# Two model blocks on one core: the weight blocks start at another byte of their 64-byte lines

## The chip, the cores and the metric

The kernel runs on one core of one Trainium2 chip. The metric is the device time in microseconds (us) of one execution. Durations of single instructions are given in nanoseconds (ns). TensorE multiplies matrices; VectorE (DVE in the profile), ScalarE (ACT) and GpSimd (POOL) work on elements; SyncE (SP) issues most DMAs.

## The reference

The reference computes two transformer-like blocks one after the other on 1024 tokens of width 1024, in 32-bit floats. Cut to what matters here:

```
u = rms_norm(x) @ w_in                   # 1024 -> 3072: RG-LRU and gated linear attention
h = x + concat(ya, yb) @ w_out
h = h + sigmoid(rms_norm(h) @ w_ple_gate + b) * (p @ w_ple_proj)
x = rms_norm(h)
z = norm(x) @ w_in_2                     # three mixers: gated attention, mLSTM, S5, and gates
y = sum of gate_b * (branch_b @ proj_b);  x = x + norm(y @ w_out_2)
x = x + norm((silu(g) * u) @ ffn_w_out), [g, u] = norm(x) @ ffn_w_in
```

Nearly all of the arithmetic is in products of the activations with large weight matrices.

## The kernel before

**Products.** Each 32-bit factor is split into a high part that TensorE's one-pass format holds (float32r) and a low part with the rest. One product of full accuracy is three matrix products, high x high, high x low and low x high (`mm3`, line 2457, all issued at line 2455). In the usual form the weight is the stationary operand, 128 x 128, loaded into the array by a LDWEIGHTS; 512 columns of the activations stream past it (the moving operand). In the profile such a product reads `mm<-rh,hi`: output, moving, stationary; `rh` and `rl` are the activations' parts, `hi` and `lo` the weight's. In a few groups (`vgroup`, line 243, and `vg` in phase B) the roles are exchanged: the activations are stationary and 256 (once 280) columns of the weight block stream.

**The ring of weight blocks.** A weight arrives as a block `raw` of 128 partitions x 1024 floats by a DMA on SP's queue; ScalarE copies it to `hi` and DVE subtracts to get `lo` (`split`, line 2466). `hi` and `lo` come from a ring of four buffers each (`ring`, line 2329), `raw` from two. The class `Stream` (line 2288) holds the list of all blocks in the order of use; when a block is used up (`done`), the next in the list is made (`more`). The ring is filled in this way in four stages that `__init__` puts into the list (line 2335): phase A (`seq_a`), phase C (`seq_c`), phase B (`seq_b`) and phase F (`seq_f`). Phase F has three kinds of keys: `"p"` (the projection), `"f"` (the first matrix of the feed-forward part, with sums and differences of blocks in a fast multiplication scheme, `variant`) and `"q"` (its second matrix, `variant2`). Within `variant` and `variant2` the ring's tiles are also filled from sums (`sl`, `sc`).

**Addresses.** In the built program each partition's row of a `hi` or `lo` buffer has 4096 bytes and begins at a multiple of 64 bytes (32192, 36288, 40384, ...), and so does every moving tile (`rh`, `rl`, `tv`, `yr`, `ah`, `al`). A product takes a slice of 128 floats (512 bytes) of the row, so its stationary block begins on a 64-byte line too. Some smaller tiles lie 32 bytes into a line: `gk` and `C` in the rows below, while `mk` and `T` of the same rows begin on one. The convolution (lines 359 to 363) reads its input rows at 0, 4, 8 and 12 bytes from their start:

```
self.act(xc, xa[:, 3 : 3 + T], AF.Identity, scale=w[3], bias=self.col("conv_b", b))
for j in (0, 1, 2):
    self.stt(xc, xa[:, j : j + T], w[j], xc, ALU.mult, ALU.add)
```

The slices that the 280-column group streams begin at 0, 1120 and 2240 bytes of a row, so one in three lies 32 bytes into a line:

```
n, per, parts = (280, 3, 3) if key == ("gv", 0) else (256, 4, 2)
c = slice((k % per) * n, (k % per) * n + n)
```

**What sets the order.** TensorE's instructions stand in the order in which the program is written (`manual_schedule`); small work of the mixers is dealt between the large products by `tick` (line 2373), one portion per 2500 ns of counted product time. The Tile layer places the waits between engines.

Of the kernel before, what the change touches and what calls it, by code (L numbers as in the profile page):

```python
# [9 lines left out]
F32R = mybir.dt.float32r  # L10
# [6 lines left out]
P = 128  # L17
# [1731 lines left out]
class PhaseF:  # L1749
# [57 lines left out]
    def variant(self, n, g, v):  # L1807

        if n == 0:
            self.fetch_raws(-1)  # L1810
        hi = self.ring.tile([P, 1024], F32R, tag="hi", name=self.name("hi"))
        lo = self.ring.tile([P, 1024], F32R, tag="lo", name=self.name("lo"))
        if v[0] == "A" and len(v) == 2:
            self.split(hi, lo, self.raws["g", 2 * g + int(v[1])])
        else:
            if v == "S1":
                self.sl[g] = self.base.tile([P, T], F32, tag="rmask", name=self.name("sl"))
            for i in range(2):
                c = slice(i * H, i * H + H)
                j = 2 * g + i  # L1820
                up, s = self.raws["u", j], self.sl[g][:, c]
                gate = self.raws.get(("g", j))
                if v == "S1":
                    self.padd(s, up[:, :H], up[:, H:])
                elif v == "S2":
                    self.psub(s, s, gate[:, :H])
                elif v == "S4":
                    self.psub(s, gate[:, H:], s)
                elif v == "S3":
                    s = self.fl.tile([P, H], F32, tag="s3", name=self.name("s3"), bufs=1)  # L1830
                    self.psub(s, gate[:, :H], up[:, :H])
                else:
                    s = up[:, H:]
                (self.psplit if g < 1 and v != "A22" else self.split)(hi[:, c], lo[:, c], s)
        self.fetch_raws(n)
        return hi, lo
# [23 lines left out]
    def variant2(self, v, e):  # L1860
        n = (2 if e < 5 else 1) * H
        if v == "S1":
            s = self.sc[e] = self.sp.tile([P, n], F32, tag=f"sc{e}", name=f"sc{e}")
            a, b = self.quad(1, 0, e), self.quad(1, 1, e, "ru")
            self.add(s, a, b)
        elif v in ("S2", "S4"):
            s, a = self.sc[e], self.quad(0, v == "S4", e)
            if v == "S2":
                self.sub(s, s, a)
            else:  # L1870
                self.sub(s, a, s)
        elif v == "S3":
            s, b = self.quad(0, 0, e), self.quad(1, 0, e, "ru")
            self.sub(s, s, b)
        else:
            s = self.quad(int(v[1]) - 1, int(v[2]) - 1, e)
        hi = self.ring.tile([P, 1024], F32R, tag="hi", name=self.name("hi"))
        lo = self.ring.tile([P, 1024], F32R, tag="lo", name=self.name("lo"))
        self.split(hi[:, :n], lo[:, :n], s)
        return hi, lo  # L1880

# [409 lines left out]
class Stream:  # L2291


    def __init__(self, k):
        self.k, self.seq, self.left = k, [], {}
        self.tiles, self.next = {}, 0

    def extend(self, seq, uses):
        self.seq += seq
        self.left.update(uses)  # L2300

    def start(self):
# [2 lines left out]

    def more(self):
        if self.next < len(self.seq):
            key, src, n = self.seq[self.next]
            self.next += 1
            self.tiles[key] = src() if callable(src) else self.k.load_split(src, n)  # L2310

# [10 lines left out]
class K(PhaseA, PhaseB, PhaseC, PhaseF):  # L2322
    depth = 4

    def __init__(self, tc, a, out):
        self.tc, self.nc, self.a, self.out = tc, tc.nc, a, out
        nc = self.nc
        self.base = tc.alloc_tile_pool(name="base", bufs=1, side="left")
        self.ring = tc.alloc_tile_pool(name="ring", bufs=self.depth, side="left")
        self.mmp = tc.alloc_tile_pool(name="mmp", bufs=4, space=PSUM)  # L2330
        self.smp = tc.alloc_tile_pool(name="smp", bufs=4, space=PSUM)
        self.ws = Stream(self)
        self.fast, self.side, self.rate, self.credit = [], [], 1.0, 0.0
        self.inside, self.ns = False, 0.0
        for s in (self.seq_a, self.seq_c, self.seq_b, self.seq_f):
            self.ws.extend(*s())

        self.edge = tc.alloc_tile_pool(name="edge", bufs=1, side="right")
        self.edge.tile([P, 8], F32, name="edge")
        self.region = tc.alloc_tile_pool(name="region", bufs=1, side="right")  # L2340
        self.uid = 0
        self.consts()
# [127 lines left out]

    def load_split(self, src, n=1024):
        raw = self.raw_tile()
        hi = self.ring.tile([P, 1024], F32R, tag="hi", name=self.name("hi"))
        lo = self.ring.tile([P, 1024], F32R, tag="lo", name=self.name("lo"))
        dst = raw[:, :n]
        if len(src.shape) == 3:
            dst = dst.rearrange("p (k c) -> p k c", k=src.shape[1])
        self.nc.sync.dma_start(dst, src)
        self.split(hi[:, :n], lo[:, :n], raw[:, :n])
        return hi, lo  # L2480

    def raw_tile(self):
        return self.ring.tile([P, 1024], F32, tag="raw", name=self.name("raw"), bufs=2)
# [94 lines left out]
```

## Time and profile before

| | |
|---|---|
| median of three runs | 2267.45 us (2266.79 to 2274.45) |
| the profiled execution | 2265.43 us, span 2263.6 us |
| TensorE busy | 2192.0 us, 10998 products |
| DVE, ScalarE, GpSimd busy | 1514.4, 903.3, 394.7 us |
| granted TensorE clock, mean | 0.986 of full |
| DMA | 297.59 MB, mean 131 GB/s |

The span runs from the first to the last instruction. Products overlap (a product's 389 ns contain the time in which its last columns run through the array), so the step from one start to the next is the measure, not the mean duration. The chain of work is followed back from the last instruction, at each step to what released it.

### The profile page before, as it was taken

Reading aid. Unit: us, or ns where it says so; the run is one execution under the profiler, and the core shown is the slowest. Engines: PE = TensorE matmul, PEld = TensorE weight load, DVE = VectorE, ACT = ScalarE, POOL = GpSimd, SP = SyncE. Lnnn points to the kernel's source line nnn. Section 1 sums busy time; section 2 is a strip of 40 time slices with the busy share of each in tenths; the row PEclk is TensorE's granted clock in tenths of the full one; section 3 lists DMA queues with packets and bytes.
Section 4 is the critical chain, followed back from the end, with each engine's and each line's share of the span. In section 5 each row is a group of like instructions: output and inputs, shape, how many; then the busy total and the mean of one; then the engine's idle time right before and its main releaser. Section 6 shows DMA issues by size and latency. Waiting matters only on the chain.

```text
span 2263.6 us, 29466 instructions
## 1 busy us (share of the span) xinstructions
PE 2192.0 (97%) x10998; PEld 1807.4 (80%) x10998; DVE 1514.4 (67%) x2160; ACT 903.3 (40%) x1522; POOL 394.7 (17%) x388
## 2 busy tenths in 40 slices
PE   8999999999999999999999999999799999999896
PEld 7888788887888988878887778887578888887676
DVE  6675686777486535558555346858977676779697
ACT  5553453344255544234253222446423232334343
POOL 1000000001112200000000000011745343425245
PEclk9999999999999999999999999999899999999998
DMA  4111116321743343255454255654233222267754
GB/s 172 34 44 40 40 51 205 103 61 29 224 144 115 98 145 136 98 170 166 152 172 143 79 183 181 202 180 153 88 123 110 84 84 84 98 228 253 246 177 160
DMA packets 149815, 297.59 MB, mean 131 GB/s; under 512 B 21520, under 2 KB 43936, under 8 KB 149416
## 3 DMA queue, kind: packets, MB, share of 16 engines
q1 hardware_dynamic: 135128, 271.33, 37.2%
q0 software_dynamic: 8128, 20.07, 2.5%
q10 hardware_dynamic: 6416, 4.31, 0.7%
q8 instruction: 87, 1.43, 0.3%
q14 instruction: 56, 0.46, 0.1%
HBM read 232.55 MB, written 61.90 MB: 130 GB/s over the span
## 4 chain that ended last, share of the span: by engine, by line
PE 76%; DVE 10%; DMA 5%; issue 5%; ACT 2%; POOL 2%; SPq 0%; POOLq 0%; ACTq 0%; DVEq 0%
PE mm L2455 56%; PE sm L2455 19%; DVE lo L2423 2%; DVE al L2423 1%; PE sm L2464 1%; DVE sc L2423 1%; DMA c<-ffa 1%; DVE res L2435 1%; DVE acc L2423 1%; POOL res L1843 1%; ACT hi L2449 0%; DVE B L2435 0%; DVE rl L2435 0%; DMA raw<-in_wfo 0%; ACT C L2449 0%
## 5 line engine op out<-in xcount | busy, mean ns | idle before, releaser
L2455 PE MATMUL mm<-rh,hi 128*128 128x512 f32 x1552 | 625.6, 403 | 1.1 <-DVE res L2423 0.7
L2455 PE MATMUL mm<-rl,hi 128*128 128x512 f32 x1552 | 606.2, 391 | 1.8 <-DVE rl L2423 1.8
L2455 PE MATMUL mm<-rh,lo 128*128 128x512 f32 x1552 | 606.7, 391 | 0.0
L2455 PEld LDWEIGHTS mm<-rh,hi 128*128 128x128 f32 x1552 | 292.5, 188 | 72.8 <-issue 9.5
L2455 PEld LDWEIGHTS mm<-rh,lo 128*128 128x128 f32 x1552 | 292.2, 188 | 62.8
L2455 PEld LDWEIGHTS mm<-rl,hi 128*128 128x128 f32 x1552 | 292.7, 189 | 61.7 <-issue 3.1
L2449 ACT ACTIVATE hi<-raw 128x1024 fp32r<-128x1024 f32 (+2 forms) x189 | 182.7, 970 | 369.3 <-PE mm L2455 265.7
L2423 DVE TENSOR_TENSOR lo<-raw,hi 128x1024 fp32r<-128x1024 f32 (+2 forms) x189 | 218.4, 1159 | 112.6 <-ACT hi L2449 110.3
L2455 PE MATMUL mm<-yr,hi 128*128 128x512 f32 x384 | 118.8, 390 | 0.2 <-DVE yr L2435 0.2
L2455 PE MATMUL mm<-tv,hi 128*128 128x512 f32 x312 | 102.5, 408 | 14.0 <-DVE tv L2423 7.1
L2455 PE MATMUL mm<-hi,rh 128*128 128x256 f32 (+1 forms) x384 | 110.7, 288 | 0.0
L2455 PE MATMUL mm<-hi,rl 128*128 128x256 f32 (+1 forms) x384 | 109.2, 284 | 0.0
L2455 PE MATMUL mm<-lo,rh 128*128 128x256 f32 (+1 forms) x384 | 109.2, 284 | 0.0
L1840 POOL TENSOR_TENSOR sl<-ru 128x512 f32<-128x512 f32 x22 | 37.1, 1689 | 315.7 <-DMA ru<-in_wfi 315.7
L2538 POOL TENSOR_TENSOR hss<-hss,mhalf 128x4 f32<-128x4 f32 x16 | 16.8, 1047 | 398.2 <-DVE hss L2441 292.1
L2455 PEld LDWEIGHTS mm<-tv,hi 128*128 128x128 f32 x312 | 61.1, 197 | 31.1 <-DVE tv L2423 9.4
L2455 PEld LDWEIGHTS mm<-yr,hi 128*128 128x128 f32 x384 | 72.1, 188 | 16.1 <-DVE yr L2435 1.1
L2449 ACT ACTIVATE hi<-sl 128x512 fp32r<-128x512 f32 x66 | 39.3, 626 | 108.9 <-PE sm L2455 66.6
L2435 DVE SCALAR_TENSOR_TENSOR adaa<-adar,cact,adaa 128x512 f32<-128x512 f32 x84 | 62.8, 747 | 29.8 <-DMA adar<-in_adaw 28.9
L2455 PEld LDWEIGHTS mm<-hi,rh 128*128 128x128 f32 x384 | 73.4, 191 | 1.7 <-issue 1.2
L2455 PE MATMUL mm<-yr,lo 128*128 128x512 f32 x192 | 74.7, 389 | 0.0
L2455 PEld LDWEIGHTS mm<-hi,rl 128*128 128x128 f32 x384 | 73.5, 191 | 0.7 <-issue 0.2
(526 smaller groups left out, 4356.7 us busy)
## 6 DMA issues: line engine op xcount, KB each, us to landing
raw<-in_w SPq DMA_DIRECT2D x60, 512.0 KB
adar<-in_adaw SPq DMA_DIRECT2D x96, 256.0 KB
c<-ffa SPq DMA_DIRECT2D x88, 256.0 KB
raw<-in_wfo SPq DMA_DIRECT2D x40, 512.0 KB
raw<-in_wfi SPq DMA_DIRECT2D x30, 512.0 KB
raw<-in_wo SPq DMA_DIRECT2D x24, 512.0 KB
ru<-in_wfi SPq DMA_DIRECT2D x22, 512.0 KB
raw<-in_wpj SPq DMA_DIRECT2D x32, 256.0 KB
```

The source lines that it names most:

```text
L1840: self.nc.gpsimd.tensor_tensor(out=out, in0=a, in1=b, op=ALU.add)
L1843: self.nc.gpsimd.tensor_tensor(out=out, in0=a, in1=b, op=ALU.subtract)
L2423: self.nc.vector.tensor_tensor(out=out, in0=a, in1=b, op=op)
L2435: self.nc.vector.scalar_tensor_tensor(out=out, in0=a, scalar=s, in1=b, op0=op0, op1=op1)
L2449: self.nc.scalar.activation(out=out, in_=a, func=f, scale=scale, **kw)
L2455: self.nc.tensor.matmul(out, lhsT=l, rhs=r, start=start, stop=stop)
L2464: self.nc.tensor.transpose(out, a, self.ident[:n, :n])
L2538: self.nc.gpsimd.tensor_tensor(out=out, in0=tmp, in1=self.mhalf[:, : out.shape[1]], op=ALU.pow)
```

## The change

The ring's tiles get 1040 floats instead of 1024, and what is used of them is a view of 1024 that begins `shift` floats in. `shift` is an entry of the stream's list. It is 4 floats (16 bytes) in phase A, 12 (48 bytes) in phase C, 2 (8 bytes) in phase B, and in phase F 6 (24 bytes) for `"p"`, 1 (4 bytes) for `"f"` and 10 (40 bytes) for `"q"`. `raw` keeps its place. In the built program each engine has the same instructions in the same order as before. The tiles of pools above the ring on the left side move up by 512 bytes.

Counted in the built program, these products read a shifted block:

| stage | bytes | 512 columns, block stationary | 256 columns, block stationary | block streams |
|---|---|---|---|---|
| A | 16 | 768 | | 384 of 256 |
| C | 48 | 768 | | |
| B | 8 | 2688 | | 576 of 256, 192 of 280 |
| F, `p` | 24 | 384 | | |
| F, `f` | 4 | 1848 | | |
| F, `q` | 40 | 792 | 264 | |

```
-        hi = self.ring.tile([P, 1024], F32R, tag="hi", name=self.name("hi"))
-        lo = self.ring.tile([P, 1024], F32R, tag="lo", name=self.name("lo"))
+        hi, lo = self.ring_pair()
...
-    def extend(self, seq, uses):
-        self.seq += seq
+    def extend(self, seq, uses, shift):
+        self.seq += [item + (shift(item[0]),) for item in seq]
...
-            key, src, n = self.seq[self.next]
+            key, src, n, self.k.shift = self.seq[self.next]
...
-        for s in (self.seq_a, self.seq_c, self.seq_b, self.seq_f):
-            self.ws.extend(*s())
+
+        f = {"p": 6, "f": 1, "q": 10}
+        shifts = (lambda key: 4), (lambda key: 12), (lambda key: 2), (lambda key: f[key[0]])
+        for s, shift in zip((self.seq_a, self.seq_c, self.seq_b, self.seq_f), shifts):
+            self.ws.extend(*s(), shift)
...
+    def ring_pair(self):
+
+        t = (self.ring.tile([P, 1040], F32R, tag=q, name=self.name(q)) for q in ("hi", "lo"))
+        return [v[:, self.shift : self.shift + 1024] for v in t]
```

The first replacement stands three times, in `variant`, `variant2` and `load_split`.

## Rows read from the trace of the kernel before

**Rows 1.** The page, busy us (share of the span) and instructions of each engine.

```profile
PE 2192.0 (97%) x10998; PEld 1807.4 (80%) x10998; DVE 1514.4 (67%) x2160; ACT 903.3 (40%) x1522; POOL 394.7 (17%) x388
```

**Rows 2.** The page, the chain that ended last, by engine and line.

```profile
PE 76%; DVE 10%; DMA 5%; issue 5%; ACT 2%; POOL 2%; SPq 0%; POOLq 0%; ACTq 0%; DVEq 0%
PE mm L2455 56%; PE sm L2455 19%; DVE lo L2423 2%; DVE al L2423 1%; PE sm L2464 1%; DVE sc L2423 1%; DMA c<-ffa 1%; DVE res L2435 1%; DVE acc L2423 1%; POOL res L1843 1%; ACT hi L2449 0%; DVE B L2435 0%; DVE rl L2435 0%; DMA raw<-in_wfo 0%; ACT C L2449 0%
```

**Rows 3.** Busy time in two stretches; then the chain's shares from 2006 to 2211.

```profile
core 0: us, PE busy (x) PEld busy (x) DVE busy (x) ACT busy (x) POOL busy (x), PEclk, DMA share, GB/s
1700.00:2000.00 300.00, 300.00 (x1325) 248.43 (x1324) 216.61 (x279) 92.87 (x145) 118.37 (x96) 1.00 0.28 92
2006.00:2211.00 205.00, 187.09 (x798) 150.53 (x797) 168.18 (x170) 79.25 (x121) 84.17 (x51) 0.97 0.71 239
...
by line: issue 19.5%; DVE al L2423 15.4%; PE mm L2455 14.0%; DVE sc L2423 8.5%; DMA c<-ffa 7.9%; PE sm L2455 7.7%; DVE lo L2423 7.1%; DVE acc L2423 3.8%; DMA ru<-in_wfo 2.8%; DMA raw<-in_wfo 2.4%; DVE yw L2423 2.1%; DMA X<-x3d 1.9%; POOL c 
```

**Rows 4.** The chain from 1700 to 1800, in order of time: start, us, what.

```profile
1701.52 2.72 PE mm L2455 x12
1704.24 2.72 PE sm L2455 x12
1706.96 2.72 PE mm L2455 x12
```

**Rows 5.** Products of 256 columns in order of time: start, us, engine, line.

```profile
2219.10 0.28 PE L2455 MATMUL mm<-ah,lo 128*128 128x256 f32 x1
...
2221.50 0.28 PE L2455 MATMUL mm<-al,hi 128*128 128x256 f32 x1
```

**Rows 6.** A stretch at half clock: busy time, PEclk; its products in time.

```profile
1215.90:1218.03 2.13, 2.13 (x6) 0.50 0.62 190
...
1215.90 0.63 PE L2455 MATMUL mm<-rl,hi 128*128 128x512 f32 x1
...
1218.03 0.60 PE L2455 MATMUL mm<-rh,hi 128*128 128x512 f32 x1
```

**Rows 7.** Ten steps after an interruption by small products, in order of time.

```profile
1208.96 0.40 PE L2455 MATMUL mm<-rl,hi 128*128 128x512 f32 x1
...
1211.27 0.39 PE L2455 MATMUL mm<-rh,lo 128*128 128x512 f32 x1
```

**Rows 8.** Products of 280 columns, each 24th, in order of time.

```profile
605.80 0.29 PE L2455 MATMUL mm<-hi,rh 128*128 128x280 f32 x1
...
608.90 0.29 PE L2455 MATMUL mm<-hi,rh 128*128 128x280 f32 x1
...
612.00 0.29 PE L2455 MATMUL mm<-hi,rh 128*128 128x280 f32 x1
```

**Rows 9.** Groups on ACT and DVE: busy us, mean ns, idle before.

```profile
L2449 ACT ACTIVATE hi<-raw 128x1024 fp32r<-128x1024 f32 x149 | 157.1, 1058 | 282.2 <-PE mm L2455 196.6 <-issue 25.7 <-PE sm L2455 25.6
...
L2449 ACT ACTIVATE T<-D,fc,hc 128x1024 f32<-128x1024 f32 x4 | 5.0, 1245 | 0.1
...
L2449 ACT ACTIVATE T<-D,cols 128x1024 f32<-128x1024 f32 x4 | 4.9, 1230 | 0.0
...
L2423 DVE TENSOR_TENSOR lo<-raw,hi 128x1024 fp32r<-128x1024 f32 x149 | 188.7, 1270 | 97.1 <-ACT hi L2449 94.8 <-PE sm L2464 2.0
...
L2435 DVE SCALAR_TENSOR_TENSOR T<-D,cols,T 128x1024 f32<-128x1024 f32 x12 | 15.3, 1277 | 0.0
...
L2435 DVE SCALAR_TENSOR_TENSOR w<-w,cols,e 128x1024 f32<-128x1024 f32 x4 | 5.1, 1279 | 2.1 <-ACT w L2449 2.1
```

**Rows 10.** Groups of weight loads: busy us, mean ns, idle before.

```profile
L2455 PEld LDWEIGHTS sm<-mq,mk 64*128 64x128 f32 x64 | 8.3, 186 | 5.3 <-issue 5.0 <-ACT C L2449 0.4
...
L2464 PEld LDWEIGHTS sm<-ident,C 128*128 128x128 f32 x64 | 7.9, 140 | 2.3 <-ACT rh L2449 0.5
L2455 PEld LDWEIGHTS sm<-gq,gk 64*128 64x128 f32 x64 | 7.4, 188 | 1.4 <-issue 1.1 <-DVE w L2423 0.4
...
L2464 PEld LDWEIGHTS sm<-ident,T 128*128 128x128 f32 x32 | 3.6, 141 | 0.3
```

More of the change, by code (lines that the diff above doesn't have):

```diff
@@ L1876, in variant2 @@
             s = self.quad(int(v[1]) - 1, int(v[2]) - 1, e)
-        hi = self.ring.tile([P, 1024], F32R, tag="hi", name=self.name("hi"))
-        lo = self.ring.tile([P, 1024], F32R, tag="lo", name=self.name("lo"))
+        hi, lo = self.ring_pair()
         self.split(hi[:, :n], lo[:, :n], s)
@@ L2472, in load_split @@
         raw = self.raw_tile()
-        hi = self.ring.tile([P, 1024], F32R, tag="hi", name=self.name("hi"))
-        lo = self.ring.tile([P, 1024], F32R, tag="lo", name=self.name("lo"))
+        hi, lo = self.ring_pair()
         dst = raw[:, :n]
```

## The prediction

> **What bounds the kernel now.** I read the busy times first, then the chain of work that ended last, then the chain by stage, and last the single matrix products in order of time, because the change touches nothing but where their operands lie. TensorE is busy for 97% of the span, its weight loads for 80% [rows 1]. A busy TensorE says little where products overlap, so the chain decides: 76% of it is TensorE, and three quarters of that are the products named `mm` and written at line 2455 [rows 2]. In the middle of the last phase, from 1700 to 2000 us, TensorE is never idle while DVE works 217 of 300 us [rows 3], so there only a shorter step from product to product can shorten the kernel. From 2006 to 2211 us the chain is a mixture in which TensorE's two pieces are 22% [rows 3]: what products save there is mostly not seen.
>
> How long is such a step? Twelve products of 512 columns take 2.72 us, which is 226.7 ns from one start to the next [rows 4]. Twenty products of 256 columns take 2.40 us, 120.0 ns each [rows 5]. The 256 further columns cost 106.7 ns, so a column costs 0.417 ns and a product has a fixed part of 13.3 ns, whichever its length. That fixed part is the only thing in the step that a different address could lower. It is not a plain constant of the engine: with the granted clock at half, five steps from 1215.90 to 1218.03 us take 426 ns each, which is just twice 213 ns of columns with nothing left over [rows 6]. So it shows only when the columns are read at full pace, which points to how the operands are fetched. It is not always 13.3 ns either. In the ten steps that follow an interruption by small products, a step is 231 ns, a fixed part of 17.7 [rows 7]; with 280 columns 24 products take 3.10 us, twice over, which leaves 12.5 ns [rows 8]. Between two interruptions the same instructions fall back to exactly 226.7.
>
> One more thing is in these numbers. 226.7 is 34 times 6.67 ns, 120.0 is 18 times 6.67 ns, and the 3.10 us of the 280-column group are 465 times 6.67 ns: settled steps are whole multiples of the time in which 16 columns, 64 bytes of a row, pass. I take 6.67 ns as the size of a step down or up (an estimate from rows 4, 5 and 8).
>
> **The change part by part.** It removes and adds no instruction, and each engine has its instructions in the same order; the pools on the left side start 512 bytes (eight lines) higher, so that no other tile changes its place within a line. What changes is the first byte of the split weight blocks.
>
> The splits: most are of 1024 elements, 1058 ns each on ScalarE and 1270 ns on DVE [rows 9]; they now write (and DVE also reads) from 4 to 48 bytes into a line. The convolution reads its input 12 bytes past such a start at `xa[:, 3:]` and takes 1230 ns on ScalarE, against 1245 ns for the same kind of operation on an input that starts on or halfway into a line; on DVE the taps at 0, 4 and 8 bytes past it have 1277 ns, against 1279 ns for a neighbour 32 bytes in [rows 9]. I take nothing. A write at such a place is not in the trace; the bounds are -15 and +15 ns (the difference just named) for each of the 149, 2.2 us, and it lies under the products: DVE has 83 idle us in the 300 us of rows 3. Without that cover it would be those 2.2 us.
>
> The weight loads as such: 64 rows of 128 columns take 188 ns where the block starts 32 bytes into a line (`gk`) and 186 ns where it starts on one (`mk`); for transposes it is 140 ns at 32 bytes (`C`) and 141 on the line (`T`) [rows 10]. Halfway into a line a load costs nothing more, so a ninth line costs none. Distances that are no multiple of 32 bytes are not in the trace, and all six of the change are of that kind. A load has 227 ns of a 512-column product to hide in, so up to 38 ns more would still be covered; with 256 columns the step is already shorter than the 188 ns of a load, and 264 such products have a shifted stationary block, all in a stretch where TensorE is not the chain.
>
> The steps of the products: 8,664 products read a shifted block (7,248 of 512 columns, 1,224 of 256 and 192 of 280; counted in the built program). With the chain's 76% I count 6,585 of them on the path. One step of 6.67 ns for each is 43.9 us. The trace gives both ends: without a fixed part, as at half clock, it is 13.3 x 6,585 = 88 us less; if a product went on for good as in the ten steps after an interruption, it is 4.3 x 6,585 = 28 us more, and one whole step up is 44 us more. Which of them? Rows 7 and 8 show that the fixed part depends on how the reading of columns and the loading of the next block happen to meet, and that a group with another length settles lower (12.5) than 13.3. Six distances give six new ways to meet. I take it that stages with half of the products on the path settle one step lower and the others stay where they are: 22 us. The sum for the profiled execution is 2265.4 - 22 = 2243.4 us; the median of the runs shown, 2267.45, is 2.0 us above the profiled one, so I forecast 2245 us. Rows 3 say that the next engine in line has room for it: DVE's 217 us fit into 300 less 3%.
>
> [...]
>
> **The rivals.** First, no change: the loads read by themselves, a load has 38 ns to spare, and the place of a stationary block is seen by nobody. For it: rows 10, and rows 9 for the other engines. Against it: a fixed part that vanishes at half clock and wanders from 12.5 to 17.7 ns with the same instructions. Left then are the 1,152 products whose shifted block is the one that streams (384 at 16 bytes, 768 at 8): one more 64-byte piece each is at most 6.67 x 1,152 = 7.7 us. Time 2267 to 2275, taken as 2269.
>
> Second, slower: the even pace is lost. In rows 7 a product that starts out of step takes 231 ns until the row of them falls into 226.7, and all blocks and moving tiles of this kernel start on 64-byte lines. If with shifted blocks they do not fall into step, every product keeps the 17.7 ns: 28 us more, 2295. It decides from the point where more products lose the pace than gain a step, about 60 against 40 in a hundred at 4.3 and 6.67 ns. For it: the pace of rows 4 is exact over hundreds of products, and so rests on something that fits. Against it: the 280-column blocks, of which each third starts 32 bytes into a line, do not fit and still have a smaller fixed part.
>
> [...]
>
> **How the numbers follow.** The forecast, faster, has 0.42; no change 0.31; slower 0.27. A change of 0.5%, 11 us, is about what a measurement can tell, so faster is below 2256, slower above 2279. By itself the first case spans 2212 (all stages a step lower, and the 264 products at the end too) to 2256. The whole range is 2212 to 2300: the upper end holds the lost pace with a little of the streaming blocks' 7.7 us. Left out are two steps for everything (2179) and a whole step up (2311), together 2 in 10.
>
> **What would show it.** In the changed profile the chain from 1700 to 2000 us should have pieces of twelve products with 2.64 us in place of 2.72 (220.0 ns) where the step is lower, 2.72 where nothing changed, 2.77 or more where the pace is lost. Each stage has its own distance, so the stages should differ if the place matters: 16 bytes first, then 48, 8, 24, 4, 40. The mean load should stay near 188 ns and ScalarE's 1058 and DVE's 1270 ns as they are. The forecast is wrong if twelve products have 2.72 us in every stage, or if single loads grow beyond the 227 ns of a step, which would make the loads the bound, a case for which nothing speaks in rows 10.

## The result and the profile after

The changed kernel takes 2288.26 us (median of four runs, 2284.35 to 2289.0) against 2267.12 us: a ratio of 1.0087, 95% interval 1.0057 to 1.0116. It is slower by about 20 us; the forecast was 2245. The profiled execution takes 2288.49 us with a span of 2286.5 us, 22.9 us longer than the span before.

The page of the changed kernel: busy times, then the chain that ended last by engine, then by line.

```profile
PE 2219.9 (97%) x10998; PEld 1805.9 (79%) x10998; DVE 1515.2 (66%) x2160; ACT 904.1 (40%) x1522; POOL 392.5 (17%) x388
...
PE 82%; DVE 8%; DMA 3%; issue 3%; POOL 2%; ACT 1%; SPq 0%; POOLq 0%; DVEq 0%; ACTq 0%
PE mm L2456 61%; PE sm L2456 20%; PE sm L2465 2%; DMA c<-ffa 1%; DVE al L2424 1%; DVE lo L2424 1%; DVE sc L2424 1%; DVE acc L2424 1%; DVE res L2436 1%; POOL res L1842 1%; DVE rl L2436 0%; DVE B L2436 0%; DMA ffa<-c 0%; ACT hi L2450 0%; DMA raw<-in_wfo 0%
```

TensorE alone has grown, 27.9 us more for the same 10,998 products [rows 1]; its weight loads, DVE, ScalarE and GpSimd are within 2.2 us of before. Its share of the chain rose from 76% to 82%, and issue, DMA and DVE each lost two points [rows 2]: part of the longer products fills time in which the chain used to wait. The granted TensorE clock was higher, 0.989 in the mean against 0.986 before:

```profile
core 0: 2286.5 us, clock 0.989
```

The two stretches of [rows 3] in the changed kernel, with the same columns:

```profile
1700.00:2000.00 300.00, 300.00 (x1297) 243.31 (x1296) 208.24 (x271) 88.11 (x139) 122.05 (x100) 1.00 0.28 93
2006.00:2211.00 205.00, 191.83 (x807) 151.60 (x806) 163.23 (x162) 75.49 (x113) 77.57 (x48) 0.98 0.71 232
```

In the first, TensorE is busy without a gap at full clock, as before, but gets 1,297 products done where it did 1,325: 2.1% fewer. The chain there, from 1700 to 1800 us (start, us, what), answers to [rows 4]:

```profile
1702.30 2.78 PE mm L2456 x12
1705.08 2.79 PE sm L2456 x12
1707.87 2.80 PE mm L2456 x12
1710.68 2.79 PE sm L2456 x12
```

Twelve products take 2.78 to 2.80 us in place of 2.72, so 231.7 to 233.3 ns each in place of 226.7. The weight loads of these products, those of `mk` and `gk`, and the two splits (busy us, mean ns | idle before):

```profile
L2456 PEld LDWEIGHTS mm<-rh,hi 128*128 128x128 f32 x1552 | 291.7, 188 | 76.8 <-issue 9.0
...
L2456 PEld LDWEIGHTS sm<-mq,mk 64*128 64x128 f32 x64 | 8.3, 186 | 5.5 <-issue 5.5
...
L2456 PEld LDWEIGHTS sm<-gq,gk 64*128 64x128 f32 x64 | 7.4, 188 | 1.5 <-ACT C L2450 0.4 <-DVE g L2424 0.4 <-ACT dec L2450 0.4
...
L2450 ACT ACTIVATE hi<-raw 128x1024 fp32r<-128x1024 f32 x149 | 157.2, 1058 | 297.1 <-PE mm L2456 207.9 <-PE sm L2456 28.5 <-issue 26.5
...
L2424 DVE TENSOR_TENSOR lo<-raw,hi 128x1024 fp32r<-128x1024 f32 x149 | 191.3, 1287 | 100.0 <-ACT hi L2450 99.6
```

A load has 188 ns as before, ScalarE's split 1058; DVE's has 1287 against 1270 [rows 9], 2.6 us in sum, which lie under the products. So no operation that touches a shifted block has become longer to speak of. What has grown is the step of the products from one start to the next.

To see on what it depends, I put each product of the trace beside its operands' addresses in the built program. Two addresses matter, as it turned out: that of the tile that streams, and that of the block that is loaded meanwhile for the next product. Their **distance** here is the second minus the first, modulo 256 bytes. In the kernel before it is 0 for 7,092 of the 7,094 products of 512 columns that are followed by a block from the ring: all ring buffers, and all tiles that stream there but a few, lie 192 bytes beyond a multiple of 256. In the changed kernel it takes many values, and not only through the shifts: the tiles of 1040 floats have 4160 bytes in place of 4096, so each buffer of the ring lies 64 bytes further (modulo 256) than its neighbour.

This is visible where phase B streams `yr`. Rows of the changed kernel, each 24 products, one block, after the one above (start, us):

```profile
1352.35 0.39 PE L2456 MATMUL mm<-yr,lo 128*128 128x512 f32 x1
...
1357.95 0.39 PE L2456 MATMUL mm<-yr,lo 128*128 128x512 f32 x1
...
1363.49 0.40 PE L2456 MATMUL mm<-yr,lo 128*128 128x512 f32 x1
...
1369.04 0.40 PE L2456 MATMUL mm<-yr,lo 128*128 128x512 f32 x1
...
1374.64 0.39 PE L2456 MATMUL mm<-yr,lo 128*128 128x512 f32 x1
```

The blocks take 5.60, 5.54, 5.55 and 5.60 us; in the built program their distances are 72, 8, 200 and 136 bytes. At 226.7 ns a block would take 5.44.

Taken product by product, the 7,278 steps of 512 columns that are under 250 ns in both profiled executions grew by 32.5 us together. All other steps together came out 10 us shorter: less waiting between products, and less time at half clock (53 us in the changed kernel's profile, 64 before; among all the kernels here it is 47 to 72).

### The profile page after: what moved, and what is told of

Same layout as the page of the kernel before. It is cut to its first block, busy times and chain, and to the rows that moved or that the text cites. A ratio compares the mean times of both kernels' runs of the same rounds, so it can differ in the third digit from the quotient of the medians.

```text
span 2286.5 us, 29468 instructions
## 1 busy us (share of the span) xinstructions
PE 2219.9 (97%) x10998; PEld 1805.9 (79%) x10998; DVE 1515.2 (66%) x2160; ACT 904.1 (40%) x1522; POOL 392.5 (17%) x388
## 4 chain that ended last, share of the span: by engine, by line
PE 82%; DVE 8%; DMA 3%; issue 3%; POOL 2%; ACT 1%; SPq 0%; POOLq 0%; DVEq 0%; ACTq 0%
PE mm L2456 61%; PE sm L2456 20%; PE sm L2465 2%; DMA c<-ffa 1%; DVE al L2424 1%; DVE lo L2424 1%; DVE sc L2424 1%; DVE acc L2424 1%; DVE res L2436 1%; POOL res L1842 1%; DVE rl L2436 0%; DVE B L2436 0%; DMA ffa<-c 0%; ACT hi L2450 0%; DMA raw<-in_wfo 0%
## 5 line engine op out<-in xcount | busy, mean ns | idle before, releaser
L2424 DVE TENSOR_TENSOR lo<-raw,hi 128x1024 fp32r<-128x1024 f32 (+2 forms) x189 | 222.1, 1178 | 116.7 <-ACT hi L2450 116.4
```

The source lines that it names most:

```text
L2424: self.nc.vector.tensor_tensor(out=out, in0=a, in1=b, op=op)
```

## The experiments

The table holds all kernels: the ratio of time to the kernel before (95% interval), the products that the profile counts from 1700 to 2000 us, the mean undisturbed step (from one start to the next, under 250 ns) of the products of 512 columns with a block from the ring, and the mean step (under 150 ns) of those of 256 columns where the block streams and where it is loaded.

| kernel | ratio | products | 512, ns | 256, block streams / is loaded, ns |
|---|---|---|---|---|
| before | 1 | 1325 | 227.4 | 119.8 / 119.9 |
| after | 1.0087 (1.0057 to 1.0116) | 1297 | 232.1 | 119.1 / 118.9 |
| pad only | 1.0057 (1.0036 to 1.0077) | 1303 | 230.9 | 118.3 / 116.9 |
| half line | 1.0143 (1.0117 to 1.0170) | 1287 | 233.4 | 118.4 / 118.1 |
| scan | 2285.29 us, one run | | 231.4 | 118.3 / 116.9 |
| read off | 1.0093 (1.0072 to 1.0114) | 1294 | 231.2 | 119.8 / 119.9 |
| ring + 64 bytes | 1.0113 (1.0091 to 1.0136) | 1288 | 233.3 | 117.3 / 114.2 |
| ring + 256 bytes | 0.9990 (0.9975 to 1.0005) | 1325 | 227.4 | 119.8 / 119.9 |
| moving + 64 bytes | 1.0113 (1.0087 to 1.0140) | 1287 | 233.3 | 117.3 / 114.5 |
| both + 64 bytes | 1.0000 (0.9982 to 1.0019) | 1326 | 227.4 | 119.8 / 119.9 |
| thirds | 0.9999 (0.9990 to 1.0008) | | 227.4 | 119.8 / 120.0 |
| thirds, 192 bytes in | 0.9989 (0.9979 to 0.9999) | | 227.4 | 116.4 / 119.9 |
| thirds, 64 bytes in | 0.9995 (0.9982 to 1.0008) | | 227.4 | 117.3 / 120.0 |

**Pad only.** The larger tiles of the change, and no shift:

```
-        shifts = (lambda key: 4), (lambda key: 12), (lambda key: 2), (lambda key: f[key[0]])
+        shifts = (lambda key: 0,) * 4
```

> The ring's tiles have 1040 floats and every distance is 0, so that only the spacing of the buffers (4160 bytes instead of 4096) and the 512 bytes of the pools above are left of the change. Theory (the place of the weight block in its 64-byte line, against that of the streamed tile, decides the step): 2267 us, twelve products of 512 columns in 2.72 us. Rival (the spacing or the moved pools do it): 2288 us, 2.78 to 2.80 us.

Measured 2281.17 us. My main theory, that the place in the 64-byte line does it, is refuted as the whole cause: no block here leaves its line's start, and some two thirds of the loss remain (0.57% of 0.87%). The same stretch of `yr`, each 24 products after the one above:

```profile
1390.28 0.39 PE L2455 MATMUL mm<-yr,lo 128*128 128x512 f32 x1
...
1395.88 0.40 PE L2455 MATMUL mm<-yr,lo 128*128 128x512 f32 x1
...
1401.36 0.39 PE L2455 MATMUL mm<-yr,lo 128*128 128x512 f32 x1
...
1406.85 0.40 PE L2455 MATMUL mm<-yr,lo 128*128 128x512 f32 x1
...
1412.44 0.40 PE L2455 MATMUL mm<-yr,lo 128*128 128x512 f32 x1
```

The four blocks, at distances 64, 0, 192 and 128, take 5.60, 5.48, 5.49 and 5.59 us. Over the whole run the undisturbed steps at distance 0, 192, 128 and 64 have means of 228.3, 229.3, 232.7 and 233.3 ns. The same instruction in the same stream changes its step with the buffer that it finds.

**Half line.** All blocks 32 bytes into their lines, in the larger tiles:

```
+        shifts = (lambda key: 8,) * 4
```

> Every block begins 8 floats (32 bytes) into its line. If any place off the line disturbs the pace: about 2288 us, steps of 231 to 233 ns. If the pace fits every 32 bytes, as the single loads at 32 bytes and the 280-column group suggest: 2267 us and 226.7 ns.

Measured 2301.9 us, the slowest of all and slower than either expectation: with the padding the distances are 32, 96, 160 and 224, and none is a good one (means of 233.0 to 233.9 ns). That a block 32 bytes into a line is harmless, as `gk` had suggested for the load alone [rows 10], is refuted for the step.

**Scan.** Distances of 0 to 15 floats in turn, in the larger tiles, upwards over the blocks of `"f"` and downwards over those of the gates (`"zg"`):

```
+            n = d.setdefault(key, len(d))
+            return n * 16 // 77 if key[0] == "f" else 15 - n * 16 // 24
```

> The 77 blocks of the feed-forward's first matrix take the distances 0 to 15 floats in turn, 4 to 5 blocks (some 115 products) each; the 24 gate blocks of phase B take 15 to 0; everything else lies on the line. One profile gives the step by distance. Theory of a lost pace: 226.7 ns at 0 alone (or at 0 and 8), 231 to 233 at all others, little difference among them. Rival that a part line costs a further fetch: 233.3 at 1 to 15 alike. If one distance is better than the line, its step is under 226.7, as 220.0.

One run: 2285.29 us. With the padding the distances go from 0 to 252 bytes in steps of 4; most have one block of 24 products, or a few. In rows of twelve products no distance has a mean step under 226.7 ns. Most settle between 230 and 233.5, one (212) near 236.7; a few beside 0 (120, 132, 156, 240 and 252 bytes) reach 226.7. So the step is not a smooth function of the distance, and 0 is not the only good value: the theory of the expectation, 226.7 at 0 alone, fails too. Where a distance stands in the scan and in the changed kernel, they agree: 226.7 ns at 240, 230.0 at 176, 230.6 at 200, 231.1 at 152 and 233.3 at 16 in both.

**Read off.** The ring of before, written at the line's start; only the slices that TensorE reads begin one float later, except the last slice of a row. Its products are therefore others than the reference's:

```
-        c = slice(k * P, k * P + P)
+        o = k * P + (k * P + P < w[0].shape[1])
+        c = slice(o, o + P)
```

> The blocks are written on the line as before, but most 128-column slices are read one float further on (all but the last of a block in the large products of phases A, B and C and of the projection, three in four in the feed-forward's first matrix); the products are those of neighbouring columns, so the output is another one. Theory (reading by the weight load): 2280 to 2288 us, steps of 231 ns or more where slices are off. Rival (ScalarE's and DVE's writes to places off the line disturb TensorE): 2267 us and 226.7 ns.

Measured 2288.73 us: where TensorE reads is enough, and the writes of ScalarE and DVE are not needed for the loss. The steps have means of 232.5 ns at a distance of 4 bytes and 228.7 at 0.

**Four moves by whole lines.** These settle whether the place itself or the distance counts. Unused tiles are put ahead of the ring (left side), or the unused tile ahead of the moving tiles (right side) is made larger; nothing else changes, and every block keeps its place in its 64-byte line.

```
+        self.base.tile([P, 16], F32, name="pad")     # ring + 64; [P, 64]: ring + 256; [P, 48] in "both"
-        self.edge.tile([P, 8], F32, name="edge")
+        self.edge.tile([P, 24], F32, name="edge")    # moving tiles 64 bytes lower; also in "both"
```

In "both" the ring lies 192 bytes higher and the moving tiles 64 lower, so that the distance is 0 again modulo 256, at another place.

> The kernel before with one unused tile of 64 bytes ahead of the ring, so that all weight blocks stay on their 64-byte lines and 4096 bytes apart, but lie one line (64 bytes) further from the streamed tiles, counted modulo 256 bytes. Theory A (distance between the loaded block and the streamed tile modulo 256 decides; in the run with spacing alone, products at 64 bytes had 233.3 ns): 233.3 ns, 2295 to 2305 us; products of 256 columns get shorter, 113 to 115 ns. Theory B (only the place within the 64-byte line counts): 2267 us and 226.7 ns.

> As before, but the unused tile has 256 bytes: the ring and the pools above it lie 256 bytes higher, the distance modulo 256 is 0 as in the kernel before. Theory A: 2267 us, 226.7 ns, 120.0 ns for 256 columns. Theory C (it is the moving of ring or pools as such that costs): slower than 2275 us.

> The weight blocks stay where they are in the kernel before, and the tiles of the right side, among them all streamed ones, lie 64 bytes lower (an unused tile of 96 bytes instead of 32 at the end). Distance 64 modulo 256. Theory A: as with the ring 64 bytes up, 233.3 ns, 2295 to 2305 us. Theory D (the weight block's own address decides, wherever the streamed tile lies): 2267 us, 226.7 ns.

> Streamed tiles 64 bytes lower and the ring 192 bytes higher: both at 128 modulo 256 where both were at 192, distance 0 again. Theory A: 2267 us, 226.7 ns, 120.0 ns. Theory D, or any that goes by absolute places: 2280 us or more.

Measured 2294.05, 2264.92, 2294.43 and 2268.29 us. Busy times from 1700 to 2000 us, in this order:

```profile
1700.00:2000.00 300.00, 300.00 (x1288) 241.70 (x1287) 208.95 (x273) 86.03 (x135) 122.92 (x102) 1.00 0.26 91
```

```profile
1700.00:2000.00 300.00, 300.00 (x1325) 248.51 (x1324) 219.98 (x284) 93.21 (x145) 114.94 (x96) 1.00 0.28 93
```

```profile
1700.00:2000.00 300.00, 300.00 (x1287) 241.65 (x1286) 208.78 (x274) 86.73 (x137) 123.45 (x102) 1.00 0.27 93
```

```profile
1700.00:2000.00 300.00, 300.00 (x1326) 248.48 (x1325) 213.66 (x279) 91.72 (x144) 118.85 (x96) 1.00 0.28 96
```

Moving either side by 64 bytes costs 1.1%; moving the ring by 256, or both sides so that the distance comes back, costs nothing that the runs can tell. So neither the ring's place nor the moving tiles' counts, but their distance, and it counts modulo 256 bytes (128 is no period: "pad only" has 232.7 ns there). Theory A's times, 2295 to 2305 us, were missed by 1 us on the low side; its 113 to 115 ns for 256 columns came where the block is loaded (114.2 and 114.5), not where it streams and the distance is 192 (117.3). In the chain of "ring + 64" the lost pace is as even as the old one:

```profile
1706.55 2.80 PE sm L2456 x12
1709.35 2.80 PE mm L2456 x12
1712.15 2.80 PE sm L2456 x12
```

2.80 us for twelve is 233.3 ns, 35 times 6.67, where 226.7 is 34 times.

At half clock a distance of 64 costs nothing. In the same kernel, at that distance, eleven steps take 4.69 us with the granted clock at 0.50; nine lie between the two rows, 426.7 ns each, as at distance 0 in [rows 6]:

```profile
1648.45:1653.14 4.69, 4.69 (x12) 0.50 0.24 85
...
1648.45 0.63 PE L2456 MATMUL mm<-tv,lo 128*128 128x512 f32 x1
...
1652.29 0.63 PE L2456 MATMUL mm<-tv,lo 128*128 128x512 f32 x1
```

**Thirds.** In the runs with a distance of 64 the 256-column products became faster at 64 (114.2 and 114.5 ns) and 192 (117.3) than at 0 (119.9 and 119.8). The last three kernels try to use that: in the groups whose block streams in 256 columns (960 products) the weights come as three blocks of 768, 768 and 512 columns, so that they can lie 0 (control), 48 or 16 floats into their buffers while all other products keep distance 0.

```
-                    wh, wl = w[k // 4]
+                    wh, wl = w[k // 3]
...
+        hi, lo = hi[:, o:], lo[:, o:]                # in load_split; o = 0, 48 or 16 for these blocks
```

> The kernel before, but each group whose weight block streams in 256 columns takes it as three blocks (768, 768 and 512 columns) instead of two of 1024; all blocks start at their buffers' first byte, distance 0 as before. It is the control for the next two. Theory A (the distance between loaded and streamed tile sets the step): 256-column products stay at 120 ns, time 2267 give or take the two more loads per group (up to +5 us, if TensorE waits for them). Rival (256-column products owe their shorter time in the shifted kernels to their place in the ring): some other step already here.

> The same three blocks, but they lie 48 floats (192 bytes) into their buffers, so that the streamed block and the loaded activations are 64 bytes apart modulo 256; all other products keep distance 0. Theory A: the 960 products of 256 columns (phases A and B) take about 115 ns instead of 120, some 5 us less in sum, so 2 to 5 us less than e9, near 2263 if e9 is at 2267; 512-column steps stay at 227.4. Rival (only distances of the 512-column kind matter, and the gain of 256 columns came with the lost pace around them): the same time as e9.

> As e10, but 16 floats (64 bytes) into the buffers: distance 192 modulo 256. Theory A by the steps seen so far (118.0 ns at this distance): 2 ns for each of 960 products, 2 us less than e9 at most. Rival as for e10: the same time as e9.

Measured 2269.68, 2265.49 and 2267.66 us (before: 2268.44). In the first such group, 60 products lie between the two rows of each kernel, in the order 0, 48, 16:

```profile
61.79 0.28 PE L2461 MATMUL mm<-lo,rh 128*128 128x256 f32 x1
...
68.99 0.28 PE L2461 MATMUL mm<-lo,rh 128*128 128x256 f32 x1
```

```profile
61.49 0.28 PE L2461 MATMUL mm<-hi,rh 128*128 128x256 f32 x1
...
68.29 0.28 PE L2461 MATMUL mm<-hi,rh 128*128 128x256 f32 x1
```

```profile
61.49 0.28 PE L2461 MATMUL mm<-hi,rh 128*128 128x256 f32 x1
...
68.55 0.28 PE L2461 MATMUL mm<-hi,rh 128*128 128x256 f32 x1
```

That is 120.0, 113.3 and 117.7 ns a step. The mean over all of them with 48 floats is 116.4 against 119.8, so 3.4 ns for 960 products, 3.3 us; the measured ratio, 0.9989 (0.9979 to 0.9999), is 2.5 us (0.2 to 4.8). So the gain is barely told from none (against its own control the medians differ by 4.2 us, and "ring + 256" has a ratio of 0.9990 without any gain in its steps); what is shown is the shorter step. That 16 floats help is not shown by its time.

## Why the prediction was wrong

**The step that failed** is the last of the sum: "stages with half of the products on the path settle one step lower". No product of 512 columns did: their mean step went from 227.4 to 232.1 ns. No kernel here, at any distance tried, has a settled step under 226.7 ns with 512 columns. The 13.3 ns beyond the columns were taken as a cost that a new address might lower as well as raise; for 512 columns the kernel before already stood at the lowest value that was found. What I read as a sign of room below was the smaller fixed part of the 280-column group [rows 8], "settles lower". That group does not settle: its loaded and streamed blocks stand at distances of 0, 64 and 160 in turn, and single steps go from 124 to 133 ns in a pattern that repeats every 24 products. 3.10 us for 24 are 19.4 times 6.67 ns for one, so by its own row the group did not fit the whole multiples that the prediction found. The thirds kernels show that room in groups of another length can be real (113.3 ns with 256 columns), but it says nothing about 512.

**The rival that came true** is the second: the even pace is lost. Its sign came, 2.78 to 2.80 us for twelve products. Its mechanism was half right: the products do not stay out of step with 17.7 ns each, as it had it; they fall into another step that goes with the distance, in "ring + 64" as even as the old one (twelve products in 2.80 us, again and again). That its price, 4.3 ns for each of 6,585 products or 28 us, lies near the 4.7 ns that were measured (232.1 less 227.4) is luck: 4.3 came from ten steps at distance 0, and the measured mean changes with the mix of distances, from 3.5 ns in "pad only" to 6.0 in "half line".

That 76% of the products stand on the path is not what the runs showed either. Nearly all products paid: 4.7 ns for 7,248 products of 512 columns are 34 us, and the undisturbed steps grew by 32.5. The span grew by 22.9 because 10 us came back in shorter waits and in the clock: all four runs of the changed kernel were granted 0.988 or 0.989 in the mean, the 27 runs of the kernel before that stand beside the last three kernels 0.983 to 0.987. How much of the 10 us is each one's is not shown. What comes back differs from kernel to kernel: "ring + 64 bytes" would pay 5.9 x 7,248 = 43 us, less 4 for the shorter 256-column products, of which its ratio of 1.0113 shows 26, two thirds; "half line" 43 less 2, of which 1.0143 shows 32, more than three quarters.

**The larger pitch of the ring was left out.** "What changes is the first byte of the split weight blocks", says the prediction; that each buffer also lies 64 bytes further from its neighbour modulo 256 is in none of its terms. It says of the pools that "no other tile changes its place within a line": true, but the line was the wrong unit. Padding alone costs 0.57% where the whole change costs 0.87%, shifting alone (read off) 0.93%; they don't add up, and both do the same, they move distances away from 0. The lower end of its range does not come out of its terms: 2267 less 43.9 for all stages, less 1.8 for the 264 products at the end, is 2222, not 2212.

**No change** (the first rival) rested on loads and streams that do not see each other, which no row of the kernel before shows. The loads' own 188 ns agree; the products' steps do not: they follow the distance between what is loaded and what streams, 227.4 ns at a distance of 0 (before) against 233.3 at 64 ("ring + 64") with the same instructions. (In "read off" nothing but the reading by TensorE changes, and its steps have 232.5 ns at a distance of 4, so the loss needs no change in where the blocks are written.)

**The stages** were to differ if the place mattered, and hardly did: 231.6 (4 bytes), 231.8 (24), 232.0 (48), 232.1 (8), 232.6 (16) and 232.8 ns (40). The padding sends each stage through four distances 64 bytes apart, which averages its own shift away. Within the stage at 4 bytes the four differ clearly: 227.2 ns at 132, 232.3 at 4, 233.1 at 196 and 233.6 at 68.

**What held:** the loads keep 188 ns, ScalarE's split 1058; DVE's split gained 17 ns, 2 more than my bound, under cover (in kernels whose blocks are written on the line it has 1270 to 1280, so not all of it need come from the shift). At a granted clock of 0.50 no fixed part shows, as the prediction read from rows 6: a step of 512 columns takes 426.7 ns at a distance of 0 and of 64, twice the 213.3 that rows 4 and 5 give for the columns at full clock. **What held in part:** 233.3 ns, one 6.67 ns above 226.7, is the commonest lost step, but settled steps are not all multiples of 6.67 ns: in "pad only" rows of twelve have 228.9 at distance 192 and 232.6 at 128, and several distances of the scan have 230.0.

**What stays open:** why the period is 256 bytes, and what makes the step longer. A product with no load beside it was not tried, so that the load takes part is concluded from the distances alone. In nearly all products the block in use and the one being loaded have the same distance, and the few steps where they differ point both ways, so it is not shown which of the two loads counts.

## What to carry to other kernels

When a tile's pitch or start changes, compare the distance between what TensorE loads and what it streams before and after, not only each tile's own alignment: padding a ring by 64 bytes lengthened the mean step of 512 columns from 227.4 to 230.9 ns, 1.5%, although every address stayed on a 64-byte line. In a stretch where TensorE is never idle, read the step from the chain's pieces of twelve products; a busy share of 97% hides it. And if a regular pace is found, first ask whether a change can only break it, for each length of product by itself.

## What the hardware showed beyond that

- The step of 32-bit (float32r) products depends on the distance between loaded block and streamed tile modulo 256 bytes: 226.7 ns at 0 and 233.3 at 64 for 512 columns, and the other way round for 256 columns, 120.0 at 0 and 113.3 at 64.
- These steps are 34, 35, 18 and 17 times 6.67 ns, one such unit up or down; other distances settle in between (228.9 ns at 192 and 232.6 at 128 in "pad only").
- At half clock a distance of 64 costs nothing: a step of 512 columns takes 426.7 ns at distance 0 (before) and at 64 ("ring + 64").
- At the same distance two paces can settle: with 48 floats (distance 64), the groups of 256 columns ran at 113.3 ns in some stretches and near 118 in others (mean 116.4).
